# Two-layer hybrid denoiser on one core: second pass of the attention scores in TensorE's two row halves

## The chip, the cores and the metric

The program runs on one core of a Trainium2 chip. The core has a matrix engine (TensorE, PE in the profile; its weight loads are the separate row PEld), a vector engine (DVE), a scalar engine (ACT), GpSimd (POOL) and SyncE (SP), which issues the transfers. The metric is the device time of one execution in microseconds (us). Before the change three runs gave 2963.67, 2968.34 and 2970.11 us, median 2968.34.

## The reference, cut to what matters

Two layers act on 1024 latent and 256 context tokens of width 1024. Each layer projects its normalised input into three mixers: differential attention (4 heads, each with two 64-wide query/key maps and a 128-wide value), a state-space scan (SSD) and a retention. Their outputs go through an output projection and are added to the input. The change is in the attention scores:

```
def diff_attention(q, k, v, lam):
    s = jnp.einsum('bqhmd,bkhmd->bhmqk', q, k).astype(jnp.float32) * (ATT_QK_DIM ** -0.5)
    p = jax.nn.softmax(s, axis=-1)
    a = p[:, :, 0] - lam * p[:, :, 1]
    return jnp.einsum('bhqk,bkhe->bqhe', a.astype(v.dtype), v)
```

The keys are 1280 per head: 1024 latent and 256 context. Queries of the context (needed in the first layer alone) see the 256 context keys only.

## The kernel before, in words

Products run on TensorE in a one-pass 32-bit format. Precision comes from splitting a factor into a high part, rounded to that format, and a low part, the rest (`split`, L275 on ACT and L277 on DVE or GpSimd). A dense product takes three passes, high by high, high by low and low by high (`mm3`, L303 where the weight is stationary, 512 or 256 columns; L305 where the activation is stationary, 256 columns).

The keys of one head and map are prepared in `head_prep`. For each group of four token tiles, a tile `khl` gets the 64 high parts and the 64 low parts of a key side by side; a transpose on TensorE (L149) puts them into `kT`, 128 rows by 1280 tokens: rows 0 to 63 high, rows 64 to 127 low. `head_a` does the same for a query tile of 128 tokens, but writes one part twice: a transposed column block of `qT` holds the high part in both row halves, the next holds the low part in both. One matmul over 128 rows then sums query-high by key-high and query-high by key-low; a second one sums query-low by both.

`head_b` computes the scores of one query tile and one map: for each chunk of keys (512, 512 and 256 columns) it takes a PSUM buffer `s`, issues the two matmuls (L924) and a row maximum on DVE (L926). The three maxima become one negated maximum `nb` (L931), and three exponentials on ACT (L936) read the PSUM buffers and free them. There are three `s` buffers in all, shared with the scans. `head_c1` to `head_c3` mix the two maps (L951, L954), transpose the result (L149) and multiply by the values (L975).

`head_loop` runs over the query tiles: 8 latent tiles and, in the first layer, 2 context tiles, for 4 heads and 2 layers. So there are 2 layers x 4 heads x 8 tiles x 2 maps = 128 calls of `head_b` with all three chunks, and 16 with the last chunk alone. In between, `yield` hands over to the stream of dense products (`phase`, `pump`), so that TensorE has other work while a tile's softmax runs. The order in which each engine finally executes is set when the program is built: the tile framework reorders the instructions by a timeline of its own, so the order in the source text is not the order on the engine.

Elsewhere in the kernel two places use a part of the array. The retention's L1111 has 64 rows of operands (one head's 64-wide half of `rkT` and `rqT`) against 128 columns; it gives 4 to 12 such matmuls in a row. The SSD's L778 writes two halves of 64 output columns side by side.

Of the kernel before, what the change touches and what calls it, by code (L numbers as in the profile page):

```python
# [52 lines left out]
class Net:  # L53
# [23 lines left out]
        self.alive = False  # L77
        self.x1k = {}

# [1 line left out]
    def nm(self, s):  # L81
        self.uid += 1
        return f"{s}_{self.uid}"
# [22 lines left out]
    def pso(self):  # L106
        return self.ps_o.tile([P, 512], F32, tag="o", name=self.nm("o"))

# [1 line left out]
    def copy(self, out, in_, eng=None):  # L110
        nc = self.nc
        if eng is None:
            self.flip ^= 1
            eng = "a" if self.flip else "v"
        if eng == "a":
            nc.scalar.activation(out=out, in_=in_, func=AF.Copy)
        elif eng == "v":
            nc.vector.tensor_copy(out=out, in_=in_)  # L118
        else:
            nc.gpsimd.tensor_copy(out=out, in_=in_)  # L120
# [29 lines left out]
            sink(i, n, ps)  # L150
            i += n

# [1 line left out]
    def setup(self):  # L154
        nc, a = self.nc, self.a
        self.ident = self.const("ident", [P, P])
        nc.sync.dma_start(out=self.ident, in_=a["ident"])
        self.ones = self.const("ones", [P, 1])
        nc.vector.memset(self.ones, 1.0)
# [45 lines left out]
        nc.vector.tensor_scalar(out=cols[:, 0:56], in0=cols[:, 0:56], scalar1=0.5, scalar2=None, op0=ALU.mult)  # L205
        return cols, cols

# [1 line left out]
    def silu_c(self):  # L209
        nc = self.nc  # L210
        cc = self.work("cc", (P, KT, 2))
        nc.sync.dma_start(out=cc, in_=self.a["cc"])
        th = self.work("cth", (P, KT, 2))
        nc.scalar.activation(out=th, in_=cc, func=AF.Tanh, scale=0.5)
        nc.vector.scalar_tensor_tensor(out=th, in0=th, scalar=1.0, in1=cc, op0=ALU.add, op1=ALU.mult)
        nc.vector.tensor_scalar(out=th, in0=th, scalar1=0.5, scalar2=None, op0=ALU.mult)
        self.sc = self.const("sc", [P, KT, 4], F32R)
        nc.vector.tensor_copy(out=self.sc[:, :, 0:2], in_=th)
        nc.vector.tensor_tensor(out=self.sc[:, :, 2:4], in0=th, in1=self.sc[:, :, 0:2].bitcast(F32), op=ALU.subtract)
        self.pick = self.const("pick", [4, 2])  # L220
        nc.vector.tensor_tensor(out=self.pick, in0=self.ident[0:4, 0:2], in1=self.ident[0:4, 2:4], op=ALU.add)
# [24 lines left out]
                op0=ALU.add, op1=ALU.add)  # L246
            yield 2.0

# [1 line left out]
    def load_w(self, src, eng="g"):  # L250
        nc = self.nc
        hi = self.w_p.tile([P, KT, 256], F32R, tag="wh", name=self.nm("wh"))
        lo = self.w_p.tile([P, KT, 256], F32R, tag="wl", name=self.nm("wl"))
        self.stage_w(src, hi, lo, 2, eng)
        return hi, lo
# [34 lines left out]
            self.prefetch()  # L290
        return w

# [1 line left out]
    def mm3(self, ps, wh, wl, ah, al, w_first):  # L294
        nc = self.nc
        n = len(wh)
        for k in range(n):
            for j, (w, x) in enumerate(((wh[k], ah[k]), (wh[k], al[k]), (wl[k], ah[k]))
                                       if w_first else
                                       ((wh[k], ah[k]), (wl[k], ah[k]), (wh[k], al[k]))):  # L300
                st, sp = (k == 0 and j == 0), (k == n - 1 and j == 2)
                if w_first:
                    nc.tensor.matmul(ps, lhsT=w, rhs=x, start=st, stop=sp)  # L303
                else:
                    nc.tensor.matmul(ps, lhsT=x, rhs=w, start=st, stop=sp)  # L305
# [50 lines left out]
        self.nc.scalar.activation(out=out, in_=ps, func=AF.Tanh, scale=0.5)  # L356
        self.nc.vector.scalar_tensor_tensor(out=out, in0=out, scalar=1.0, in1=ps, op0=ALU.add, op1=ALU.mult)  # L357

# [1 line left out]
    def defer(self, n, fn):  # L360
        self.later.append([n, fn])

# [33 lines left out]
                break  # L396
            used += r

# [1 line left out]
    def new_act(self, c):  # L400
        n = CHUNKS[c][1]
        h = self.act_p.tile([P, KT, n], F32R, tag=f"ah{c}", name=self.nm("ah"))
        l = self.act_p.tile([P, KT, n], F32R, tag=f"al{c}", name=self.nm("al"))
        self.act[c] = (h, l)
        return h, l
# [64 lines left out]
            self.sumsq_add(acc, xs[k], k, n, self.nc.gpsimd if c else None)  # L470
        return acc

# [1 line left out]
    def conv_evac(self, t, idx, cv, edge, c, n, ps):  # L474
        nc = self.nc
        w = [cv[:, 3 * idx + j:3 * idx + j + 1] for j in range(3)]
        t0 = CHUNKS[c][0]
        nc.scalar.activation(out=t[:, t0:t0 + n], in_=ps, func=AF.Identity, bias=cv[:, 36 + idx:37 + idx],
                             scale=w[1])
        nc.vector.scalar_tensor_tensor(out=t[:, t0 + 1:t0 + n], in0=ps[:, 0:n - 1], scalar=w[0],  # L480
                                       in1=t[:, t0 + 1:t0 + n], op0=ALU.mult, op1=ALU.add)
        nc.vector.scalar_tensor_tensor(out=t[:, t0:t0 + n - 1], in0=ps[:, 1:n], scalar=w[2],
                                       in1=t[:, t0:t0 + n - 1], op0=ALU.mult, op1=ALU.add)
        if c == 0:
            nc.vector.tensor_copy(out=edge, in_=ps[:, n - 1:n])
        if c == 1:
            nc.vector.scalar_tensor_tensor(out=t[:, t0:t0 + 1], in0=edge, scalar=w[0],
                                           in1=t[:, t0:t0 + 1], op0=ALU.mult, op1=ALU.add)
            nc.vector.scalar_tensor_tensor(out=t[:, t0 - 1:t0], in0=ps[:, 0:1], scalar=w[2],  # L489
                                           in1=t[:, t0 - 1:t0], op0=ALU.mult, op1=ALU.add)  # L490
# [359 lines left out]
        r = self.mean_rsqrt(pt[:, 0:m], m, 512)  # L850
        self.copy(self.rg[:, g, 0:m], r, "v")

# [1 line left out]
    def rope(self, x):  # L854
        nc = self.nc
        for i in range(0, NLT, 4):
# [26 lines left out]
    def head_prep(self, h, last):  # L883
        nq = NLT if last else NT
        k, = self.need(f"k{h}")
        self.qk_norm(k, self.r["kn"][:, 0:64], NT)
        yield
        self.rope(k)
        yield
        kT = []  # L890
        for m in range(2):
            t = self.unit("kT", (P, TOK), F32R)
            for i in range(0, NT, 4):
                n = min(4, NT - i)
                hl = self.work("khl", (P, n, 2, 64), F32R)
                self.split(k[:, i:i + n, 64 * m:64 * m + 64], hl[:, :, 0, :], hl[:, :, 1, :], "v")
                self.transposes([hl[:, j].rearrange("p s d -> p (s d)").bitcast(F32) for j in range(n)],
                                lambda _, n, ps: self.copy(t[:, i * P:(i + n) * P], ps[:, 0:n * P]))
            kT.append(t)
            yield  # L900
        q, = self.need(f"q{h}")
        self.qk_norm(q, self.r["qn"][:, 0:64], nq)
        yield
        self.rope(q)
        self.heads[h] = (q, kT)
        yield
# [9 lines left out]

    def head_b(self, qT, kT, m, z, chunks):
        nc = self.nc
        pss = []
        mx = self.tiny("mx", 3)  # L920
        for ci, (t0, n) in enumerate(chunks):
            ps = self.pss()
            for s in range(2):
                nc.tensor.matmul(ps[:, 0:n], lhsT=qT[:, 2 * m + s, :], rhs=kT[m][:, t0:t0 + n],  # L924
                                 start=(s == 0), stop=(s == 1))
            nc.vector.tensor_reduce(out=mx[:, ci:ci + 1], in_=ps[:, 0:n], axis=AX.X, op=ALU.max,  # L926
                                    negate=len(chunks) == 1)
            pss.append(ps)
        if len(chunks) > 1:
            nb = self.tiny("nb", 1)  # L930
            nc.vector.tensor_reduce(out=nb, in_=mx[:, 0:3], axis=AX.X, op=ALU.max, negate=True)  # L931
        else:
            nb = mx[:, 0:1]
        em = self.unit("e")
        for ci, (t0, n) in enumerate(chunks):
            nc.scalar.activation(out=em[:, t0:t0 + n], in_=pss[ci][:, 0:n], func=AF.Exp, bias=nb,  # L936
                                 accum_out=z[:, 3 * m + ci:3 * m + ci + 1])
        return em
# [103 lines left out]
                nc.sync.dma_start(out=self.mix[dst, :, 0:n * P], in_=g[:, 0:n * P])  # L1042
            yield

# [1 line left out]
    def ret_mix(self, pr, last):  # L1046
        nc = self.nc
        nq = NLT if last else NT
# [79 lines left out]
            self.post = self.finish_head(O, ssq, f"rg{h}", nq, 12 + h, 1)  # L1128
            yield base + 0.45

# [1 line left out]
    def load_mix(self, c, tiles, cols, scaled):  # L1132
        nc = self.nc
        t0, n = CHUNKS[c]
# [108 lines left out]
                else:  # L1243
                    self.posts = {0: post}

# [1 line left out]
    def w_order(self, l):  # L1247
        wi, wa = self.a["wi"], self.a["wa"]
        q = [(wa[0, i], "gv") for i in ADA0] if l == 0 else []
        late = iter([(wa[0, i],) for i in range(8, 12)] + [(wa[1, i],) for i in range(12)])  # L1250
        for i in range(N_W):
            q.append((wi[l, i], "gv" if i < 2 else "g"))
            if l == 0 and 10 <= i < N_W - 1:
                q += itertools.islice(late, LATE[i - 10])
        q += [(self.a["wo1"][l, i],) for i in range(4)]
        q += [(self.a["wo2a"][l, i],) for i in range(2)]
        return q
# [233 lines left out]
```

## Time and profile before

| what | value |
|---|---|
| median of three runs | 2968.34 us (2963.67 to 2970.11) |
| the profiled execution: first to last instruction | 2963.4 us |
| PE busy (matmul) | 2683.0 us, 91% |
| DVE, ACT, POOL busy | 1992.9, 1277.0, 1191.2 us |
| matmuls of the scores (L924) | 800, of these 512 of 512 columns |
| mean granted TensorE clock | 0.954 of 2.4 GHz |

The profiled execution has no separate time on the page; its span is 0.3 us under the fastest of the three runs and 4.9 us under their median. A busy PE is not PE at its peak, since matmuls overlap in its pipeline and their ends are modelled. What a matmul costs in a dense stretch is therefore the distance from its start to the next one's start in the timeline, not its duration there. A timeline row gives the start and the length in us, the engine, the line, the operation, out<-in, then active rows and columns of the array (128*128, 64*128 or 128*64), the moving operand's shape, and how many instructions the row merges. Idle time and what ended it stand in square brackets.

### The profile page before, as it was taken

Reading aid. Unit: us, or ns where it says so; the run is one execution under the profiler, and the core shown is the slowest. Engines: PE = TensorE matmul, PEld = TensorE weight load, DVE = VectorE, ACT = ScalarE, POOL = GpSimd, SP = SyncE. Lnnn points to the kernel's source line nnn. Section 1 sums busy time; section 2 is a strip of 40 time slices with the busy share of each in tenths; the row PEclk is TensorE's granted clock in tenths of the full one; section 3 lists DMA queues with packets and bytes.
Section 4 is the critical chain, followed back from the end, with each engine's and each line's share of the span. In section 5 each row is a group of like instructions: output and inputs, shape, how many; then the busy total and the mean of one; then the engine's idle time right before and its main releaser. Section 6 shows DMA issues by size and latency. Waiting matters only on the chain.

```text
span 2963.4 us, 47064 instructions
## 1 busy us (share of the span) xinstructions
PE 2683.0 (91%) x17708; PEld 2352.7 (79%) x17708; DVE 1992.9 (67%) x4409; ACT 1277.0 (43%) x3297; POOL 1191.2 (40%) x910
## 2 busy tenths in 40 slices
PE   6887988779899989998999989997899999999999
PEld 4666777669788879897878777775798888989887
DVE  7668778765767785657445558888658767665651
ACT  5345555443545454523132345545435444452330
POOL 5546656662423231325240336666531211212550
PEclk8988999889999999999999989998999999999999
DMA  6022222221211111204462122222110100001461
GB/s 236 13 69 81 80 76 67 82 67 43 58 44 52 44 53 29 68 27 122 135 216 79 39 73 79 72 78 72 58 43 15 37 15 22 29 24 36 148 211 60
DMA packets 128339, 211.23 MB, mean 71 GB/s; under 512 B 12080, under 2 KB 53232, under 8 KB 128112
## 3 DMA queue, kind: packets, MB, share of 16 engines
q1 hardware_dynamic: 128112, 208.23, 22.5%
q8 instruction: 139, 2.28, 0.3%
q14 instruction: 88, 0.72, 0.1%
HBM read 172.47 MB, written 35.72 MB: 70 GB/s over the span
## 4 chain that ended last, share of the span: by engine, by line
PE 53%; DVE 13%; issue 5%; ACT 3%; DMA 2%; POOL 1%; SPq 0%; DVEq 0%; POOLq 0%; ACTq 0%
PE mm L303 23%; PE mm L305 13%; PE t L149 4%; PE o L975 4%; PE s L924 4%; DVE mx L926 2%; DVE te L747 2%; PE o L778 1%; ACT e L936 1%; DVE e L954 1%; POOL wl L277 1%; DVE mt L744 1%; PE s L710 1%; DMA raw<-in_wi_dram 1%; DVE mt L752 1%
## 5 line engine op out<-in xcount | busy, mean ns | idle before, releaser
L277 POOL TENSOR_TENSOR wl<-raw,wh 128x512 fp32r<-128x512 f32 x288 | 391.5, 1380 | 705.8 <-ACT wh L275 699.0
L303 PE MATMUL mm<-ah,wh 128*128 128x512 f32 (+1 forms) x1680 | 635.3, 378 | 41.2 <-DVE cv L489 7.6
L303 PE MATMUL mm<-al,wh 128*128 128x512 f32 (+1 forms) x1680 | 626.9, 373 | 1.0 <-DVE al L277 1.0
L303 PE MATMUL mm<-ah,wl 128*128 128x512 f32 (+1 forms) x1680 | 626.2, 373 | 0.0
L305 PE MATMUL mm<-wh,ah 128*128 128x256 f32 x1568 | 455.1, 291 | 17.5 <-DVE zu L357 9.9
L305 PE MATMUL mm<-wl,ah 128*128 128x256 f32 x1568 | 451.1, 288 | 0.3 <-POOL wl L277 0.3
L305 PE MATMUL mm<-wh,al 128*128 128x256 f32 x1568 | 450.1, 287 | 0.0
L303 PEld LDWEIGHTS mm<-ah,wh 128*128 128x128 f32 x1680 | 323.9, 193 | 101.9 <-issue 19.4
L303 PEld LDWEIGHTS mm<-ah,wl 128*128 128x128 f32 x1680 | 323.7, 193 | 52.8 <-issue 2.4
L303 PEld LDWEIGHTS mm<-al,wh 128*128 128x128 f32 x1680 | 324.3, 193 | 51.6 <-issue 2.4
L305 PEld LDWEIGHTS mm<-wh,ah 128*128 128x128 f32 x1568 | 302.4, 193 | 24.0 <-DVE zu L357 10.4
L936 ACT ACTIVATE e<-s,nb 128x512 f32<-128x512 f32 (+1 forms) x384 | 231.8, 613 | 198.3 <-DVE nb L931 197.0
L305 PEld LDWEIGHTS mm<-wl,ah 128*128 128x128 f32 x1568 | 302.9, 193 | 4.3 <-issue 1.2
L305 PEld LDWEIGHTS mm<-wh,al 128*128 128x128 f32 x1568 | 302.8, 193 | 3.0 <-issue 0.9
L926 DVE TENSOR_REDUCE mx<-s 128x1 f32<-128x512 f32 (+1 forms) x400 | 223.1, 586 | 64.3 <-PE s L924 63.2
L275 ACT ACTIVATE wh<-raw 128x512 fp32r<-128x512 f32 x288 | 169.1, 625 | 173.1 <-DMA raw<-in_wi_dram 62.0
L924 PE MATMUL s<-kT,qT 128*128 128x512 f32 (+1 forms) x800 | 218.9, 377 | 10.2 <-ACT e L936 8.7
L750 POOL TENSOR_TENSOR mt<-mt,G 128x512 f32<-128x512 f32 x72 | 117.3, 1632 | 177.1 <-DVE mt L744 168.1
L747 DVE SCALAR_TENSOR_TENSOR te<-R,dtpk,te 128x128 f32<-128x128 f32 x288 | 176.0, 656 | 9.5 <-ACT te L739 9.5
L755 POOL TENSOR_TENSOR R<-R,cv 128x1024 f32<-128x1024 f32 x72 | 177.6, 2468 | 2.9 <-ACT R L754 2.9
L975 PE MATMUL o<-v,aT 128*128 128x128 f32 x1312 | 176.4, 277 | 0.7 <-DVE aT L118 0.5
L975 PEld LDWEIGHTS o<-v,aT 128*128 128x128 f32 x1312 | 165.2, 194 | 4.1 <-DVE aT L118 0.9
(265 smaller groups left out, 5182.1 us busy)
## 6 DMA issues: line engine op xcount, KB each, us to landing
raw<-in_wi_dram SPq DMA_DIRECT2D x176, 256.0 KB
R<-cumd SPq DMA_DIRECT2D x72, 512.0 KB
raw<-in_wa_dram SPq DMA_DIRECT2D x64, 256.0 KB
mr<-mix SPq DMA_DIRECT2D x64, 256.0 KB
wr<-in_wa_dram SPq DMA_DIRECT2D x32, 256.0 KB
raw<-in_wo_dram SPq DMA_DIRECT2D x32, 256.0 KB
x<-xr SPq DMA_DIRECT2D x24, 256.0 KB
mix<-cv SPq DMA_DIRECT2D x8, 640.0 KB
```

Source lines behind the costliest of these rows:

```text
L149: self.nc.tensor.transpose(ps[:, j * P:(j + 1) * P], srcs[i + j], self.ident)
L275: nc.scalar.activation(out=hi, in_=x, func=AF.Copy)
L277: e.tensor_tensor(out=lo, in0=x, in1=hi.bitcast(F32), op=ALU.subtract)
L303: nc.tensor.matmul(ps, lhsT=w, rhs=x, start=st, stop=sp)
L305: nc.tensor.matmul(ps, lhsT=x, rhs=w, start=st, stop=sp)
L747: nc.vector.scalar_tensor_tensor(out=te[:, hh, c, :], in0=Rv[:, 1, hh, c, :], scalar=col(self.ncum, c, 1, hh), in1=te[:, hh, c, :], op0=AL ...
L750: nc.gpsimd.tensor_tensor(out=mt, in0=mt, in1=G[:, c0:c0 + 2, :].unsqueeze(1).to_broadcast([P, 2, 2, P]), op=ALU.mult)
L755: nc.gpsimd.tensor_tensor(out=cs, in0=cs, in1=cT[:, tk].unsqueeze(1).to_broadcast([P, 4, 256]), op=ALU.mult)
L924: nc.tensor.matmul(ps[:, 0:n], lhsT=qT[:, 2 * m + s, :], rhs=kT[m][:, t0:t0 + n], start=(s == 0), stop=(s == 1))
L926: nc.vector.tensor_reduce(out=mx[:, ci:ci + 1], in_=ps[:, 0:n], axis=AX.X, op=ALU.max, negate=len(chunks) == 1)
L936: nc.scalar.activation(out=em[:, t0:t0 + n], in_=pss[ci][:, 0:n], func=AF.Exp, bias=nb, accum_out=z[:, 3 * m + ci:3 * m + ci + 1])
L975: nc.tensor.matmul(po[:, 0:P], lhsT=aT[j], rhs=v[:, j, :], start=(j == b0), stop=(j == NT - 1))
```

## The change

`head_prep` exchanges the halves for token tiles 4 to 7 (keys 512 to 1023): there `kT` has the low parts in rows 0 to 63 and the high parts in rows 64 to 127. The first pass sums over all 128 rows and does not see the exchange. `head_b` takes its PSUM buffers first, and for the two chunks of 512 keys replaces the second pass over 128 rows by one over 64: chunk 0 uses rows 0 to 63 and chunk 1 rows 64 to 127, where its high parts are. The products of query-low by key-low are thereby left out for those 1024 keys. The chunk of 256 keys keeps both passes. The row maxima come in a loop of their own behind all matmuls. The number of matmuls, transposes, splits, maxima and exponentials stays as it was.

```diff
@@ head_prep
                 hl = self.work("khl", (P, n, 2, 64), F32R)
-                self.split(k[:, i:i + n, 64 * m:64 * m + 64], hl[:, :, 0, :], hl[:, :, 1, :], "v")
+                z = int(i == 4)
+                self.split(k[:, i:i + n, 64 * m:64 * m + 64], hl[:, :, z, :], hl[:, :, 1 - z, :], "v")
@@ head_b
-        pss = []
         mx = self.tiny("mx", 3)
+        k = kT[m]
+        qh, ql = qT[:, 2 * m, :], qT[:, 2 * m + 1, :]
+        pss = [self.pss() for _ in chunks]
         for ci, (t0, n) in enumerate(chunks):
-            ps = self.pss()
-            for s in range(2):
-                nc.tensor.matmul(ps[:, 0:n], lhsT=qT[:, 2 * m + s, :], rhs=kT[m][:, t0:t0 + n],
-                                 start=(s == 0), stop=(s == 1))
+            nc.tensor.matmul(pss[ci][:, 0:n], lhsT=qh, rhs=k[:, t0:t0 + n], start=True, stop=False)
+            if n < 512:
+                nc.tensor.matmul(pss[ci][:, 0:n], lhsT=ql, rhs=k[:, t0:t0 + n], start=False, stop=True)
+            elif ci == 1:
+                for j in range(2):
+                    r = slice(64 * j, 64 * j + 64)
+                    nc.tensor.matmul(pss[j], lhsT=ql[r], rhs=k[r, 512 * j:512 * j + 512], start=False, stop=True)
+        for ci, (t0, n) in enumerate(chunks):
+            ps = pss[ci]
             nc.vector.tensor_reduce(out=mx[:, ci:ci + 1], in_=ps[:, 0:n], axis=AX.X, op=ALU.max,
                                     negate=len(chunks) == 1)
-            pss.append(ps)
```

In the changed kernel the first passes have line L925, the second pass of the last chunk L927 and the half passes L931; L975 of before is L982. The built order of TensorE shows where they stand. First, layer 0, head 0, the second map of the first query tile, in a stretch with dense products (L305) around it; before:

```order
L924 MATMUL s_6369<-kT_6136,qT_6263 128x512 x2
...
L924 MATMUL s_6373<-kT_6136,qT_6263 128x512 x2
L305 MATMUL mm_6557<-wh_5743,ah_1078 128x256
L305 MATMUL mm_6557<-wl_5744,ah_1078 128x256
L305 MATMUL mm_6557<-wh_5743,al_1079 128x256
L924 MATMUL s_6377<-kT_6136,qT_6263 128x256 x2
```

and now:

```order
L925 MATMUL s_6369<-kT_6136,qT_6263 128x512
L931 MATMUL s_6369<-kT_6136,qT_6263 128x512
L305 MATMUL mm_6557<-wl_5744,ah_1078 128x256
L305 MATMUL mm_6557<-wh_5743,al_1079 128x256
L305 MATMUL mm_6557<-wh_5743,ah_1078 128x256
L305 MATMUL mm_6557<-wl_5744,ah_1078 128x256
L925 MATMUL s_6370<-kT_6136,qT_6263 128x512
L931 MATMUL s_6370<-kT_6136,qT_6263 128x512
L305 MATMUL mm_6557<-wh_5743,al_1079 128x256
```

Each half pass (L931) stands directly behind its own chunk's first pass, and the two half passes are six matmuls apart, one of them chunk 1's first pass over all rows.

Second, the same map one query tile later, without dense products between; now:

```order
L982 MATMUL o_6516<-v_693_5079,aT_6446 128x128 x2
L925 MATMUL s_6498<-kT_6136,qT_6273 128x512
L931 MATMUL s_6498<-kT_6136,qT_6273 128x512
L925 MATMUL s_6499<-kT_6136,qT_6273 128x512
L931 MATMUL s_6499<-kT_6136,qT_6273 128x512
L925 MATMUL s_6500<-kT_6136,qT_6273 128x256
L927 MATMUL s_6500<-kT_6136,qT_6273 128x256
```

Here one matmul, the first pass of chunk 1, stands between the two half passes.

Third, one of the places where the two half passes are neighbours, as the source text has them (layer 0, beside a product of L234):

```order
L234 MATMUL mm_9857<-wh_9768,sc 4x256
L925 MATMUL s_9713<-kT_8661,qT_9694 128x512
L925 MATMUL s_9714<-kT_8661,qT_9694 128x512
L931 MATMUL s_9713<-kT_8661,qT_9694 128x512
L931 MATMUL s_9714<-kT_8661,qT_9694 128x512
L925 MATMUL s_9715<-kT_8661,qT_9694 128x256
L927 MATMUL s_9715<-kT_8661,qT_9694 128x256
```

Over the whole program the 128 pairs of half passes stand so: 8 as neighbours, 42 with one matmul between (in 38 of these it is chunk 1's first pass), 78 with two or more between.

## Rows read from the trace of the kernel before

**Rows 1.** The page: busy time of each engine, and the chain that ended last by engine.

```profile
PE 2683.0 (91%) x17708; PEld 2352.7 (79%) x17708; DVE 1992.9 (67%) x4409; ACT 1277.0 (43%) x3297; POOL 1191.2 (40%) x910
PE 53%; DVE 13%; issue 5%; ACT 3%; DMA 2%; POOL 1%; SPq 0%; DVEq 0%; POOLq 0%; ACTq 0%
```

**Rows 2.** Busy time by stretch: the attention of layer 0 and of layer 1.

```profile
core 0: us, PE busy (x) PEld busy (x) DVE busy (x) ACT busy (x) POOL busy (x), PEclk, DMA share, GB/s
680.00:1260.00 580.00, 548.12 (x3965) 500.17 (x3964) 401.71 (x921) 288.95 (x835) 182.11 (x125) 0.97 0.17 50
2200.00:2660.00 460.00, 434.14 (x3101) 398.67 (x3100) 325.15 (x775) 224.80 (x679) 89.37 (x57) 0.99 0.09 25
```

**Rows 3.** Who waited for whom, longest first, in 680 to 1260 us: us, times, longest.

```profile
ACT e L936 <- DVE nb L931: 97.9, 39, 5.9
...
DVE mx L926 <- PE s L924: 41.4, 37, 4.7
```

**Rows 4.** PE's timeline in layer 1's attention: one call of head_b among dense products.

```profile
2409.43 0.63 PE L924 MATMUL s<-kT,qT 128*128 128x512 f32 x2
2409.90 0.28 PE L305 MATMUL mm<-wh,al 128*128 128x256 f32 x1
2410.02 0.27 PE L305 MATMUL mm<-wh,ah 128*128 128x256 f32 x1
```

**Rows 5.** PE's timeline in the retention: dense products, then a 64-row matmul, then transposes.

```profile
1342.27 0.39 PE L303 MATMUL mm<-ah,wh 128*128 128x512 f32 x1
...
1343.41 0.39 PE L303 MATMUL mm<-ah,wl 128*128 128x512 f32 x1
1343.73 0.71 PE L1111 MATMUL s<-rqT,rkT 64*128 64x128 f32 x4
1344.37 0.66 PE L149 MATMUL t<-ident,qs 128*128 128x128 f32 x4
```

**Rows 6.** PEld's timeline at the same place.

```profile
1343.19 0.19 PEld L303 LDWEIGHTS mm<-ah,wl 128*128 128x128 f32 x1
1343.73 0.52 PEld L1111 LDWEIGHTS s<-rqT,rkT 64*128 64x128 f32 x4 [0.35 <-issue]
```

**Rows 7.** PE's timeline: twelve 64-row matmuls after a dense product.

```profile
1295.43 1.60 PE L1111 MATMUL s<-rqT,rkT 64*128 64x128 f32 x12
1296.96 0.66 PE L149 MATMUL t<-ident,qs 128*128 128x128 f32 x4
```

**Rows 8.** PE's timeline: back from 64 rows to dense products.

```profile
1288.84 0.38 PE L305 MATMUL mm<-wh,ah 128*128 128x256 f32 x1
1289.06 0.28 PE L305 MATMUL mm<-wl,ah 128*128 128x256 f32 x1
1289.18 0.28 PE L305 MATMUL mm<-wh,al 128*128 128x256 f32 x1
```

**Rows 9.** PE's timeline in the SSD: one dense product between matmuls on column halves.

```profile
1820.43 0.44 PE L778 MATMUL o<-mt,xn 128*64 128x128 f32 x4
1820.80 0.49 PE L303 MATMUL mm<-al,wh 128*128 128x512 f32 x1
1821.23 0.44 PE L778 MATMUL o<-R,sf 128*64 128x128 f32 x4
```

## Prediction

> **What bounds the kernel now.** I read the page first. TensorE is busy for 91% of the span and holds 53% of the chain that ended last, DVE 13% [rows 1]. So it matters whether TensorE is also full where the change acts. The busy time by stretch answers that: over the two attentions PE is busy 548 of 580 us and 434 of 460 us, at 0.97 and 0.99 of the full 2.4 GHz clock [rows 2]. It stands idle 32 + 26 = 58 us of 1040, under 6%. DVE reaches about 70% there. In these stretches PE's queue is the bound, because the dense products fill it while a tile's softmax runs; time added to that queue lengthens the program, time taken out shortens it, except for what the 58 us take up.
>
> The waits are the third view. The maxima wait 41 us for the scores, and the exponentials 98 us for the maxima [rows 3]. So scores, maximum, exponential is a chain that starts at the matmuls of the change. A delay there isn't soaked up by the idle time of PE alone: the work that PE waits for afterwards comes later too.
>
> The fourth view is PE's timeline, for prices. In it, one pass of 512 columns costs (2409.90 - 2409.43) / 2 = 0.235 us beside dense products, and one of 256 columns 0.12 us [rows 4]. Dense 512-column products follow each other at (1343.41 - 1342.27) / 5 = 0.228 us [rows 5].
>
> **What the change removes, if it did what its words say.** In each of the 128 full calls of `head_b` two second passes of 512 columns would run at once instead of one behind the other. That takes one pass of 0.228 to 0.235 us from PE: 128 x 0.23 = 29 us. For this the two half passes have to be neighbours in PE's order. The built order shows that 8 of 128 pairs are. Elsewhere a matmul over all rows stands between, mostly chunk 1's first pass, and a half pass can't run beside that. So 8 x 0.23 = 1.8 us is the gain in this program as it stands.
>
> **What it adds: going into 64 rows and back.** The half passes are matmuls over 64 rows in a stream of matmuls over 128 rows. The 8 neighbouring pairs are one excursion each, the other 240 half passes one each: 248 excursions. The kernel before has the same thing in its retention, and the timeline prices it in three pieces:
>
> - Going in: the last dense product starts at 1343.41, the first 64-row matmul at 1343.73, so 0.32 us instead of 0.228: 0.09 more [rows 5].
> - Inside and on leaving: four 64-row matmuls and the step out take 1344.37 - 1343.73 = 0.64 us [rows 5], twelve take 1296.96 - 1295.43 = 1.53 us [rows 7]. Eight matmuls are thus 0.89 us, 0.111 each; four are 0.445, which leaves 0.195 us. About 0.10 of it follows the first matmul. The weight loads say why: PEld stands idle for 0.35 us at "issue", and the first 64-row weight load starts together with its matmul, where ordinarily it starts one step ahead [rows 6]. The rest, 0.09, is the step out.
> - After the return: the first dense product takes 1289.06 - 1288.84 = 0.22 us up to the next, instead of 0.12: 0.10 more [rows 8].
>
> The sum is 0.09 + 0.195 + 0.10 = 0.385 us for one excursion. A second place bears it out: a single dense product between two excursions onto column halves takes 1821.23 - 1820.80 = 0.43 us, which is 0.228 + 0.20, the return and the next way in [rows 9]. The half passes have 512 columns and another 32-bit format than these rows; I take the price to be the same, since it is the same with transposes or dense products next to it. The lower bound is that only the gaps before a start count and the weight loads are hidden: 0.09 x 2 = 0.18 us.
>
> So PE's queue grows by 240 x 0.385 = 92.4 us for the single half passes and by 8 x (0.385 - 0.228) = 1.3 us for the pairs, together 93.7 us. Even an ideal order would lose: 128 pairs side by side would be 128 x 0.157 = 20 us more than before. The change pays from an excursion under 0.23 us, and only with the pairs adjacent.
>
> **What hides it.** At most the 58 idle us. In the stretches without idle time nothing is hidden; where PE waits, it waits for DVE and ACT work that the later scores push back [rows 3]. I take a quarter of the 58, 15 us, as absorbed, between 0 and 58. That gives 93.7 - 15 = 78.7 us.
>
> **The other edits.** The exchanged halves in `head_prep` are the same splits, transposes and copies with another column offset; they cost nothing, with no cover needed. The three PSUM buffers are claimed together, but they are the same three in the same turn, and a buffer is waited for by the first matmul that writes it, so this too I cost at nothing. The maxima, maximum by maximum, stand behind the same matmuls as before. The dense products fall a few places to either side in PE's order; whether that gains or loses I can't read from the trace, and allow 10 us either way, under a fifth of the idle time.
>
> **The sum.** Profiled span 2963.4 + 78.7 = 3042 us. The median of the runs is 4.9 us above that span, so the time comes to about **3046 us**, 2.6% slower. What late scores push is late next: the maximum, the exponentials, and the transposes and value products of the following query tile.
>
> **Rivals.**
>
> 1. *Only the gaps count.* The weight load of the next matmul is hidden under the long 512-column pass. Then an excursion costs 0.18 us, PE's queue grows by 240 x 0.18 = 43 us, less 15 x 43/94 = 7 hidden: 2968 + 36 = 3004 us. For it: the rows of 64-row matmuls are of 128 columns, which leave less time to load. Against it: the weights waited behind a 512-column product too [rows 6].
> 2. *The idle time takes up most.* All 58 us go: 2968 + 36 = 3004 us. For it: a fuller PE queue means less waiting. Against it: the chain in rows 3 starts at the delayed matmuls.
> 3. *Nothing is hidden and the new order loses its 10 us:* 2968 + 94 + 10 = 3072 us.
> 4. *The change doesn't do what it says, and costs nothing either.* No price for 64 rows in this format, hardly any pair adjacent: 2968 - 2 = 2966 us. Against it: rows 5 to 9, without exception.
> 5. *Faster: the halves run at once for free.* The place is PE's queue at the second passes; the price is 0.23 us saved per pair, and the point from which it decides is an excursion under 0.23 us with the halves side by side in every call. Full gain: 2968 - 29 = 2939 us. For it: column halves do run side by side, four L778 take 0.37 us where four L1111 take 0.64 [rows 5, 9]. Against it: the built order, and the 0.385 us.
>
> On rival 5 the Trainium skill has a rule, in "TensorE: Matmul & The Clock Gate", section "Measured speedup vs the span model": matmuls in different row groups take about the time of one, plus some 4 ns for each further one. By that alone 128 pairs would save about 128 x 0.226 = 29 us, an estimate. Rows 9 agree for column halves; no run here shows it for row halves. "TensorEngine Tiling", section "Key Properties", says against it that a change of tiling mode drains the engine, without a price; the trace agrees, with 0.09 us before each start.
>
> **How the numbers follow.** Chances: forecast 0.62, rival 1 0.13, rival 2 0.10, rival 3 0.08, rival 4 0.04, rival 5 0.03. About 0.2% of the time, 6 us, is what a measurement of this kernel can tell from no change. All but rivals 4 and 5 are slower by more than that: slower 0.93, same 0.04, faster 0.03. The range runs from just under rivals 1 and 2 to rival 3: 3002 to 3070 us, leaving out rivals 4 and 5 and the ends of the others.
>
> **What would show it.** In the changed profile: half passes (L931) whose start comes about 0.32 us after a first pass's, a next matmul some 0.42 us after theirs (0.235 + 0.10 + 0.09), and weight loads of L931 that begin with their matmul, PEld idle before. The attention stretches should be longer by some 80 us together, the rest unchanged. In the 8 adjacent pairs the two starts should lie a few ns apart. The forecast is wrong if the step after a lone half pass is about 0.235 us, or if the steps are as priced but the stretches grow by less than 40 us.

## The result and the profile after

The changed kernel takes 3073.0 us (median of 4 runs, 3067.7 to 3073.2) against 2969.1 us in the same comparison: ratio 1.0354, interval 1.0338 to 1.0370, so 3.5% or some 105 us slower. Forecast were 3046 us with a range up to 3070. The sign is right, the size is outside the range by 3 us.

The changed kernel's page, busy times and the chain by engine, to compare with [rows 1]:

```profile
PE 2788.8 (91%) x17708; PEld 2359.2 (77%) x17708; DVE 2000.2 (65%) x4409; ACT 1278.5 (42%) x3297; POOL 1191.4 (39%) x910
PE 57%; DVE 12%; issue 4%; ACT 2%; POOL 1%; DMA 1%; POOLq 0%; DVEq 0%; ACTq 0%
```

PE has as many instructions as before and 106 us more busy time; DVE, ACT and POOL have as many as before too, and at most 7 us more busy time. The span grew by 102.5 us (3065.9 against 2963.4), so almost all of the loss lies in PE's queue. Its share of the chain went from 53% to 57%.

Where in the program? I cut both executions at the first and last score matmul of each layer. Busy time by stretch, before (first row of each pair: layer 0's attention, second: layer 1's; the columns are those of [rows 2]):

```profile
707.60:1254.30 546.70, 515.05 (x3691) 467.64 (x3689) 381.95 (x875) 278.70 (x805) 166.55 (x115) 0.97 0.17 50
2199.30:2655.20 455.90, 430.04 (x3064) 394.39 (x3063) 323.05 (x770) 223.05 (x673) 85.86 (x54) 0.99 0.09 26
```

and after:

```profile
711.40:1289.70 578.30, 556.04 (x3682) 462.32 (x3681) 382.85 (x872) 278.53 (x803) 168.71 (x115) 0.98 0.16 48
2243.10:2754.70 511.60, 486.08 (x3048) 399.97 (x3047) 327.24 (x768) 223.96 (x672) 84.79 (x54) 0.95 0.08 23
```

Layer 0's attention is 31.6 us longer, layer 1's 55.7 us, together 87 of 102.5; the remaining 15 lie in the three stretches outside. PE's idle time (length minus busy) fell from 31.7 to 22.3 us in layer 0 and stayed at 25.5 us in layer 1. So some of the added work did go into idle time, but only about 10 us. In layer 1 the granted clock fell from 0.99 to 0.95. The trace's clock has two levels, 2.4 and 1.2 GHz; layer 1's attention has 10 us at the lower one before and 48 us now. If PE was busy in all of the 38 us more, half speed cost at most 19 us there. That is an estimate, and a part of the 55.7 us.

PE's timeline of the changed kernel, one half pass among dense products, answers to [rows 4, 5, 8]:

```profile
2417.92 0.39 PE L925 MATMUL s<-kT,qT 128*128 128x512 f32 x1
2418.24 0.49 PE L931 MATMUL s<-kT,qT 64*128 64x512 f32 x1
2418.66 0.39 PE L305 MATMUL mm<-wh,al 128*128 128x256 f32 x1
2418.88 0.28 PE L305 MATMUL mm<-wh,ah 128*128 128x256 f32 x1
2419.00 0.28 PE L305 MATMUL mm<-wl,ah 128*128 128x256 f32 x1
```

Read the starts: 0.32 us from the first pass to the half pass, 0.42 to the next dense product, 0.22 to the one after, then 0.12 again. Three steps cost 0.96 us where two full passes and a dense step cost 0.235 + 0.235 + 0.12 = 0.59 us. The difference, 0.37 to 0.38 us, is the priced excursion. It is no picked case: 113 lone half passes of this trace stand so, at the full clock and without a wait, and their median steps are the same. PEld's timeline at the same place shows the second half of the reason:

```profile
2417.80 0.19 PEld L925 LDWEIGHTS s<-kT,qT 128*128 128x128 f32 x1
2418.24 0.18 PEld L931 LDWEIGHTS s<-kT,qT 64*128 64x128 f32 x1 [0.24 <-issue]
2418.66 0.19 PEld L305 LDWEIGHTS mm<-wh,al 128*128 128x128 f32 x1 [0.24 <-issue]
2418.77 0.19 PEld L305 LDWEIGHTS mm<-wh,ah 128*128 128x128 f32 x1
```

The weights of the full pass (L925) are loaded 0.12 us ahead of their matmul, at 2417.80 for a start at 2417.92. Those of the half pass start with their matmul, at 2418.24, and so do those of the first dense product behind it, at 2418.66. This is what [rows 6] showed for the retention.

The waits in layer 0's attention (711 to 1290 us) answer to [rows 3]:

```profile
ACT e L943 <- DVE nb L938: 104.2, 38, 7.8
DVE mx L934 <- PE s L931: 52.9, 57, 6.1
```

The maxima wait 52.9 us for the scores instead of 41.4, and the exponentials 104.2 instead of 97.9: the chain behind the scores did slip.

### The profile page after: what moved, and what is told of

Its sections match the earlier page's. It is cut to its first block, busy times and chain, and to the rows that moved or that the text cites. A ratio compares the mean times of both kernels' runs of the same rounds, so it can differ in the third digit from the quotient of the medians.

```text
span 3065.9 us, 47067 instructions
## 1 busy us (share of the span) xinstructions
PE 2788.8 (91%) x17708; PEld 2359.2 (77%) x17708; DVE 2000.2 (65%) x4409; ACT 1278.5 (42%) x3297; POOL 1191.4 (39%) x910
## 4 chain that ended last, share of the span: by engine, by line
PE 57%; DVE 12%; issue 4%; ACT 2%; POOL 1%; DMA 1%; POOLq 0%; DVEq 0%; ACTq 0%
PE mm L303 22%; PE mm L305 15%; PE o L982 5%; PE t L149 4%; PE s L931 3%; PE s L925 3%; DVE te L747 2%; PE o L778 1%; DVE mx L934 1%; DVE mt L752 1%; DVE mt L744 1%; DVE rs L1101 1%; POOL wl L277 1%; DVE mr L1150 1%; PE mm L234 1%
## 5 line engine op out<-in xcount | busy, mean ns | idle before, releaser
L305 PE MATMUL mm<-wh,ah 128*128 128x256 f32 x1568 | 461.4, 295 | 19.2 <-DVE zu L357 11.4
L305 PE MATMUL mm<-wl,ah 128*128 128x256 f32 x1568 | 456.6, 291 | 0.0
L305 PE MATMUL mm<-wh,al 128*128 128x256 f32 x1568 | 456.5, 291 | 0.0
L305 PEld LDWEIGHTS mm<-wh,ah 128*128 128x128 f32 x1568 | 306.3, 195 | 28.0 <-DVE zu L357 11.6
L305 PEld LDWEIGHTS mm<-wl,ah 128*128 128x128 f32 x1568 | 306.7, 196 | 7.5 <-issue 7.4
L305 PEld LDWEIGHTS mm<-wh,al 128*128 128x128 f32 x1568 | 306.2, 195 | 6.2 <-issue 6.2
L982 PE MATMUL o<-v,aT 128*128 128x128 f32 x1312 | 180.6, 280 | 0.0
L925 PE MATMUL s<-kT,qT 128*128 128x512 f32 (+1 forms) x400 | 164.2, 416 | 7.5 <-ACT e L943 5.9
L982 PEld LDWEIGHTS o<-v,aT 128*128 128x128 f32 x1312 | 164.8, 194 | 7.0 <-issue 5.4
```

The source lines that it names most:

```text
L925: nc.tensor.matmul(pss[ci][:, 0:n], lhsT=qh, rhs=k[:, t0:t0 + n], start=True, stop=False)
L982: nc.tensor.matmul(po[:, 0:P], lhsT=aT[j], rhs=v[:, j, :], start=(j == b0), stop=(j == NT - 1))
```

## The experiments

At this point theory A was the price of the excursions, 248 x 0.385 us less the pairs' gain, with next to nothing hidden. Against it stood an order effect (B) and a lower clock brought by the half rows (C). In the text below, differences to before are the measured ratio times 2969 us. Kernels with half rows leave out the low-by-low products of the keys concerned, as the change does.

**All rows again, in the changed order.**

```diff
-                    r = slice(64 * j, 64 * j + 64)
-                    nc.tensor.matmul(pss[j], lhsT=ql[r], rhs=k[r, 512 * j:512 * j + 512], start=False, stop=True)
+                    nc.tensor.matmul(pss[j], lhsT=ql, rhs=k[:, 512 * j:512 * j + 512], start=False, stop=True)
```

> The changed kernel with its second passes over all 128 rows again, in the new place and order (7 of 128 pairs adjacent, as good as the changed kernel's order). Theory A (the price of going into 64 rows and back, 0.385 us for each of 248 excursions): no excursion is left, so 2969 us within 6 us, like before. Rival B (the new order of dense products, buffers and maxima costs a good part of the 104 us): 2985 us or more. Rival C (the price, and besides it a lower clock that the half rows bring in layer 1's attention): 2969 us, and the time at 1.2 GHz in layer 1's attention falls from 48 us back to about 10 us.

Measured: 2985.8 us, ratio 1.0058 (1.0043 to 1.0073), 17 us over before. A alone (2969) is missed by 17 us. B's bound of 2985 is just met, but 17 of 105 us is not a good part of the loss. So 17 us come with the new order of statements, and the difference to the changed kernel, 88 us, is left for the half rows. That difference holds the built order fixed only in part: by the two traces, both kernels execute the same instructions in the same order until the middle of layer 1's attention (2521 us in the changed kernel), and behind it 1057 of PE's rows stand elsewhere. Busy time by stretch, layer 1's attention of this kernel:

```profile
2203.80:2671.20 467.40, 433.12 (x3058) 396.31 (x3057) 326.26 (x768) 223.03 (x672) 85.10 (x54) 0.98 0.09 25
```

It is 467.4 us long against 455.9 before, with PE busy for 3 us more and idle for 34 us instead of 26. Layer 0's attention has its old length (546.0 us). That is 11.5 of the 15.3 us by which this execution's span (2978.7 us) exceeds that of before. The added idle time of PE is 8.4 us, about half of the order's loss in this profile. The clock of 0.98 is some 20 us at 1.2 GHz, between the 48 and the 10 of C.

**Half rows in one layer alone.**

```diff
-                    r = slice(64 * j, 64 * j + 64)
+                    r = slice(64 * j, 64 * j + 64) if self.half else slice(0, P)
...
+        self.half = l == 0
```

The second kernel has `l == 1` in the last line.

> Half rows in layer 0 alone, all rows in layer 1. Theory A without any hiding: half of the excursions, 2969 + 47 = 3016 us. With layer 0 hiding a third, as its stretch in the changed profile says (578.3 against 546.7 us): 2969 + 32 = 3001 us. Rival C: 3001 us, and layer 1's attention back at about 456 us with 10 us at 1.2 GHz.

> Half rows in layer 1 alone. Theory A without any hiding: 2969 + 47 = 3016 us. Rival C (a lower clock comes with the half rows in layer 1): 2969 + 56 = 3025 us, with some 48 us at 1.2 GHz in layer 1's attention. If the clock there falls by chance of where the waits lie: 3005 to 3016 us, with about 10 us at 1.2 GHz.

Measured: 3026.0 us (ratio 1.0195, 1.0180 to 1.0210) and 3028.6 us (1.0210, 1.0194 to 1.0227), 58 and 62 us over before. The sums without a clock term (3001 to 3016 us) were too low; the 17 us of the order were in none of them. C's 3025 us for layer 1 is 4 us under the measured time, within the interval, though it has no order term either. Against the kernel with all rows the two layers cost 41 and 45 us; the sum of 86 us agrees with the 88 us that both together cost. Each layer holds 124 or so excursions, 47 us by the price.

Layer 0 is the cleaner of the two. By the traces, the kernel with half rows in layer 0 executes every row of PE, DVE, ACT and POOL in the order of the all-rows kernel, and the kernel with half rows in layer 1 does so in the order of the changed kernel. Each of these two pairs differs by layer 0's half rows alone, and they cost 41 and 43 us (each within some 7), 87 to 90% of the price. Layer 1's 45 us also hold the rows that moved there and the lower clock.

Layer 1's attention in the kernel with half rows in layer 0 alone, and with half rows in layer 1 alone:

```profile
2246.90:2713.70 466.80, 432.35 (x3058) 395.71 (x3057) 325.94 (x768) 222.90 (x672) 84.90 (x54) 0.98 0.09 25
```

```profile
2212.20:2723.50 511.30, 485.86 (x3047) 400.09 (x3046) 326.80 (x768) 223.86 (x672) 84.67 (x54) 0.95 0.08 23
```

The first is the all-rows length, the second the changed kernel's. The granted clock goes with it, 0.98 and 0.95, as C had it: 17 and 48 us at 1.2 GHz. By the same estimate as above up to 15 of layer 1's 45 us may be the clock's.

**Adjacent pairs.** Each half pass is tied in the built order to stand behind what precedes it in the source text.

```diff
-                    nc.tensor.matmul(pss[j], lhsT=ql[r], rhs=k[r, 512 * j:512 * j + 512], start=False, stop=True)
+                    mm = nc.tensor.matmul(pss[j], lhsT=ql[r], rhs=k[r, 512 * j:512 * j + 512], start=False, stop=True)
+                    self.tc.keep_in_program_order(mm)
```

> The half passes pinned behind chunk 1's first pass in program order: 123 of 128 pairs are adjacent, 133 excursions instead of 248. Theory A: 123 x (0.385 - 0.228) + 10 x 0.385 - 5 x 0 = 23 us over before, 2992 us; starts within a pair a few ns apart. Rival B (order): the time depends on where the dense products fall, so nothing near that sum, 2969 to 3070 us. Rival D (side by side without a price): 2969 - 28 = 2941 us.

Measured: 3051.0 us, ratio 1.0280 (1.0263 to 1.0297), 83 us over before, where A had 23. The pairs do run at once. PE's timeline of this kernel:

```profile
718.69 0.40 PE L925 MATMUL s<-kT,qT 128*128 128x512 f32 x1
719.02 0.50 PE L931 MATMUL s<-kT,qT 64*128 64x512 f32 x2
719.45 0.39 PE L305 MATMUL mm<-wh,ah 128*128 128x256 f32 x1
719.67 0.28 PE L305 MATMUL mm<-wl,ah 128*128 128x256 f32 x1
```

Both half passes fit between 719.02 and 719.45, 0.43 us, as long as one alone took above; in 119 of the 123 pairs of this trace the second starts 3 or 4 ns after the first, in the others 2 or 5. The excursion's steps are 0.33, 0.43 and 0.22 us, as priced. So the pair is not what cost 60 us more; the tie was the suspect, and needed its own control.

**The tied order with all rows.** The kernel above with `lhsT=ql, rhs=k[:, ...]`.

> The pinned order of e2 (first passes of both chunks, then both second passes, 123 of 128 pairs adjacent), but second passes over all 128 rows: e2 without its row halves. e2 took 3051 us. Theory A (an adjacent pair in row halves costs 0.385 - 0.228 us more than two passes over all rows): e2 minus 123 x 0.157 and 10 x 0.385 = 23 us, 3028 us; then the pinned order by itself costs some 60 us. Rival E (the pinned order costs no more than the changed kernel's order, and an adjacent pair costs 0.5 us more): 2986 us, as e1.

Measured: 3022.0 us, ratio 1.0176 (1.0161 to 1.0192), 52 us over before: close to A's 3028, far from the rival's 2986. The tied order by itself loses 52 us. What the half rows add to it is 83 - 52 = 31 us, where the price of 123 adjacent pairs and 10 single excursions was 23. The two intervals together leave some 7 us of room, and the difference to the price is 8: the price comes out near, but the sum is not confirmed. The two kernels' executed orders are not the same from 2381 us on, either. Busy time by stretch, the two attentions of this kernel:

```profile
707.00:1265.70 558.70, 518.26 (x3683) 468.38 (x3681) 381.56 (x873) 278.18 (x804) 167.87 (x115) 0.97 0.17 50
2220.20:2706.00 485.80, 444.52 (x3049) 406.64 (x3048) 316.89 (x768) 223.65 (x672) 80.46 (x54) 0.95 0.08 24
```

PE is idle 40 and 41 us there, against 32 and 26 before. The clock of layer 1 is 0.95 here too, without a single half row. So C is not shown as it was put: a lower clock in this stretch comes without half rows as well, and layer 0's clock did not fall with them. But with half rows in layer 1 its clock was lower each time than in the same order of statements without them, 0.95 against 0.98 and, in the old order below, 0.96 against 0.99.

**Half rows with the statements in the old order.**

```diff
             for s in range(2):
-                nc.tensor.matmul(ps[:, 0:n], lhsT=qT[:, 2 * m + s, :], rhs=kT[m][:, t0:t0 + n],
+                r = slice(64 * ci, 64 * ci + 64) if s and n == 512 else slice(0, P)
+                nc.tensor.matmul(ps[:, 0:n], lhsT=qT[r, 2 * m + s, :], rhs=kT[m][r, t0:t0 + n],
                                  start=(s == 0), stop=(s == 1))
```

The halves in `head_prep` are exchanged as in the change; those lines are left out here.

> The kernel before with halves exchanged and half rows in the second passes of the two chunks, statements in the old order (buffer, two passes, maximum, chunk by chunk). 256 excursions, no pair adjacent. Price 256 x 0.385 = 99 us, of which, as in the layers of e3 and e4 against e1, some 12% is hidden: 87 us. If the 17 us that e1 showed belong to the new order of statements, they are absent: 2968 + 87 = 3055 us. If a loss of that size comes with any other order of the same work: 3065 to 3075 us.

Measured: 3056.6 us, ratio 1.0290 (1.0275 to 1.0306), 86 us over before; 87 was expected without an order loss. The 17 us are absent. This is a second measurement of the half rows, independent of the 88 us above. Busy time by stretch, the two attentions:

```profile
708.30:1290.00 581.70, 558.80 (x3690) 463.73 (x3689) 385.23 (x875) 279.97 (x804) 166.34 (x115) 0.98 0.16 47
2235.10:2744.20 509.10, 488.31 (x3063) 402.85 (x3062) 328.63 (x770) 224.21 (x673) 82.33 (x54) 0.96 0.08 23
```

The stretches outside the attentions have their old lengths here to within 1 us (708.3, 945.1 and 308.2 against 707.6, 945.0 and 308.2), while the changed kernel lost 15 us there. The two attentions together take 1090.8 us here and 1089.9 in the changed kernel. So against this kernel the changed one's order loss shows outside the attentions, while in the all-rows kernel it showed in layer 1's. Some of those 15 us are chance: the first stretch, in which no instruction has moved, is 3.8 us longer too, and the middle one takes 948.1 us in the all-rows kernel and 953.4 in the changed kernel, in the same executed order. Where the order costs its time is therefore open.

Which of the statements' moves makes the order lose can be narrowed down from the built order alone, without a run: claiming the three buffers first, or moving the maxima behind all matmuls, leaves every row on TensorE, VectorE and ScalarE in its place. Only the second passes behind chunk 1's first pass move rows. That rows move is not yet a loss: this kernel executes 1177 of PE's 17708 rows in another place than before, the all-rows kernel 1901.

**A third half pass.** The 256-key chunk's second pass over 64 rows as well, so no key gets low-by-low products in it.

```diff
-                nc.tensor.matmul(pss[ci][:, 0:n], lhsT=ql, rhs=k[:, t0:t0 + n], start=False, stop=True)
+                nc.tensor.matmul(pss[ci][:, 0:n], lhsT=ql[0:64], rhs=k[0:64, t0:t0 + n], start=False, stop=True)
```

> The changed kernel with the second pass of the 256-key chunk over 64 rows too: 144 further excursions, none adjacent. If the price belongs to the way in and back, whatever the pass's length: 144 x 0.385 = 55 us, less 12% hidden, 49 us over the changed kernel: 3122 us. If it grows with the number of columns, half of it: 3098 us.

Measured: 3105.6 us, ratio 1.0453 (1.0435 to 1.0470), 29 us over the changed kernel, where 49 or 24 were expected. The total is nearer the second, but PE's timeline decides for the first:

```profile
719.17 0.28 PE L925 MATMUL s<-kT,qT 128*128 128x256 f32 x1
719.38 0.38 PE L927 MATMUL s<-kT,qT 64*128 64x256 f32 x1
719.69 0.38 PE L305 MATMUL mm<-wh,al 128*128 128x256 f32 x1
719.91 0.28 PE L305 MATMUL mm<-wh,ah 128*128 128x256 f32 x1
```

The steps are 0.21, 0.31 and 0.22 us, 0.74 instead of 3 x 0.12: again 0.38 us, with half the columns. The price does not grow with the length of the pass. It is in PE's queue in full: PE's busy time in the two attentions is 590.2 and 509.5 us against 556.0 and 486.1, 58 us more for 144 x 0.385 = 55. PE's idle time there took up 10 us of it. By the medians 29 us show in the time; the two profiled executions differ by 42 us (3108.0 and 3065.9), but they are the slowest of one kernel's four runs and the fastest of the other's. What became of the rest the runs don't tell.

**The price taken out of the kernel before.** Its own 4-row matmuls (L240) are excursions too. They were filled up with zeros to 128 rows:

```diff
-        self.pick = self.const("pick", [4, 2])
-        nc.vector.tensor_tensor(out=self.pick, in0=self.ident[0:4, 0:2], in1=self.ident[0:4, 2:4], op=ALU.add)
+        self.pick = self.const("pick", [P, 2])
+        nc.vector.tensor_tensor(out=self.pick, in0=self.ident[:, 0:2], in1=self.ident[:, 2:4], op=ALU.add)
+        self.adar = self.const("adar", [P, 256])
+        nc.vector.memset(self.adar, 0.0)
...
-                    nc.tensor.matmul(pt[:, 2 * j:2 * j + 2], lhsT=row[0:4, j * P:(j + 1) * P], rhs=self.pick,
+                    nc.tensor.matmul(pt[:, 2 * j:2 * j + 2], lhsT=row[:, j * P:(j + 1) * P], rhs=self.pick,
```

> The kernel before, without a half pass anywhere, but with its own 4-row matmuls (L240, the adaptive-norm columns, 24 groups of four) made 128 rows by zeros below the four rows; the order on TensorE and ScalarE is that of before, VectorE has one memset more. If going into fewer rows and back is what costs, the 24 excursions (0.09 in, 0.53 - 0.445 = 0.085 inside, 0.10 after, 0.275 us each) go: 16 lie in full queues, 8 in the start, where TensorE waits anyway: 4 to 7 us less, 2962 to 2965 us against 2969. If the price belongs to half rows of long passes only: no change.

Measured: 2965.3 us against 2966.9, ratio 0.9990, interval 0.9978 to 1.0003. The sign is the expected one, but the interval takes in no change: inconclusive. 24 excursions are too few to see in the time.

## Why the prediction was wrong, point by point

- *PE's queue is the bound in the attentions:* right. PE's busy time grew by 106 us and the span by 102.5.
- *The change doesn't do what its words say, 8 of 128 pairs adjacent:* right; the timeline has the half passes alone, as the built order did. Where pairs are adjacent they run at once, a few ns apart.
- *The price, 0.385 us for an excursion, 93.7 us in all:* right. The steps are 0.32, 0.42 and 0.22 us, as written down before. In the time, half rows cost 88 us over the same kernel with all rows, 86 us of 99 in the old order of statements, and 41 and 43 of 47 in layer 0 where the executed order was the same.
- *Rival 1, hidden weight loads:* fell. The loads start with their matmuls behind 512-column passes, too.
- *What hides it, 15 of 58 us:* less than that, within its range of 0 to 58. By the differences 6 us were hidden in the changed order (94 - 88) and 13 us in the old one (99 - 86), each within some 5 to 7 us. The lower clock in layer 1 is not taken out of these; by whatever it cost, more was hidden than they say.
- *The step that failed* is the one on the other edits: "whether that gains or loses I can't read from the trace, and allow 10 us either way". In the sum it stood at nothing. It measured 17 us (12.8 to 21.7), all of it loss. That 94 less 6 plus 17 gives 105 us is no check, since the 6 come from the same difference; the check is the old order, whose 86 us and the 17 make 103. With the 15 us hidden as forecast the order alone would have brought the sum to 3064 us, so the rest, 9 us, is what was not hidden.
- *The attention stretches longer by some 80 us, the rest unchanged:* 87 us, and 15 in the rest. The second half of this sign failed.
- *Rival 3*, nothing hidden and a lost order, had 3072 us against the measured 3073. Its shape is nearer than the forecast's, but that it fits to 1 us is luck: some 6 us were hidden, and the order lost 17, not 10.
- *The sum as written:* 2968.3 + 78.7 is 3047 us, not 3046, and the range's upper end of 3070 lies under rival 3's own 3072, to which it was said to run. Neither changes the account.
- *An ideal order would still lose:* the sum was 20 us for all pairs adjacent. The runs give 31 us, within some 7, over the tied order with all rows, so the sign is right and the size a little low. That order costs another 52 us, which the prediction had not thought of: with the passes tied, PE is idle in the attentions for 24 us more than before, not quite half of it, and layer 1's clock is lower; the rest is not explained.

Open are two things. Why the moved passes lose time, and where, is not shown: idle time of PE in layer 1 in one build, the stretches outside the attentions in the other. And what the lower clock in layer 1 (0.95 against 0.99) costs is bounded, by an estimate of at most 19 us, but not separated from the rest: it comes with half rows in layer 1, but also in the tied order without them.

No version tried here beats the kernel before by more than its measurement can tell.

## What to carry to other kernels

In this kernel, using part of the array's rows for a single matmul in a dense stream cost 0.38 us on the way in and back at the full clock, for 128, 256 and 512 columns alike; two 512-column passes side by side save 0.23 us. By these numbers row halves would pay only with two or more pairs in one excursion (2 x 0.23 against 0.385), which no run here tried. The built order, not the source text, tells whether pairs stand together. Before blaming a change's mechanism for its whole loss, run it with the mechanism undone and the statement order kept: here a sixth of the loss was the order, and tying the order cost more than it brought. Then compare the executed orders row by row, since the same statement order need not give the same built order; the two pairs of kernels that ran in one and the same order gave the cleanest price, 41 and 43 us for layer 0.

## What was not expected of the hardware

The forecast had the second half pass of an adjacent pair starting a few ns after the first. It does, 3 or 4 ns, and both take no longer than one (0.43 us to the next start). Not expected was that the price of an excursion is the same around 128-, 256- and 512-column passes, 0.38 us: it shows in the three steps around the pass, while the weight loads begin with their matmuls.

The price follows the clock. PE's timeline of the changed kernel in a stretch (1085.4 to 1088.0 us) with a granted clock of 0.50, that is 1.2 GHz:

```profile
1085.43 0.78 PE L925 MATMUL s<-kT,qT 128*128 128x512 f32 x1
1086.13 0.79 PE L931 MATMUL s<-kT,qT 64*128 64x512 f32 x1
1086.85 0.58 PE L305 MATMUL mm<-wl,ah 128*128 128x256 f32 x1
1087.23 0.41 PE L305 MATMUL mm<-wh,al 128*128 128x256 f32 x1
```

The steps are 0.70, 0.72 and 0.38 us, 1.80 together. At this clock a pass of 512 columns takes 0.43 us and one of 256 columns 0.21 to the next start (medians of this trace), so the excursion costs 0.73 us, about twice its price at 2.4 GHz (the median of six such places in this trace is 0.76).
